# adaLN's small pieces summed four steps behind their load, and the partition sums of the larger pieces seven steps behind it

## The chip, the cores and the metric

The kernel runs on one core of a Trainium2 chip. The metric is the device time of one execution in microseconds (us). TensorE (PE) does the matmuls, VectorE (DVE), ScalarE (ACT) and GpSimd (POOL) the elementwise work. SyncE (SP) issues the transfers of the weights. The queue of ACT also issues the transfers that the change is about.

## The reference

One layer of a decoder, in float32, with 1024 tokens of width 1024. A conditioning vector c gives six modulation vectors of 1024 values each (shift, scale and gate of two sub-layers), by one product with w_ada (1024 x 6144). The modulated input goes through one wide projection into two groups of heads.

```
mod = silu(c) @ w_ada + b_ada             # six vectors: shift, scale, gate (two sub-layers)
h   = rms(x) * (1 + scale1) + shift1
rq, rk, rv, fq, fk, fv, og, rg = h @ w_in # two halves of the heads in parallel
ret = retention(rope(rq), rope(rk), rv)   # in 8 chunks of 128 tokens, state carried on
fox = softmax attention(fq, fk, fv) with forget gates, gated by og
x   = x + gate1 * ([fox, ret * gate] @ w_out)
x   = x + gate2 * (relu(h2 @ w_mlp_in)**2 @ w_mlp_out)   # h2: the second modulated norm
```

The first projection needs only shift1 and scale1. The other four vectors (numbers 2 to 5 in the code) are needed later, so their pieces of w_ada are worked off beside the projections.

## The kernel before

**Projections.** Each product is made of three matmuls of split operands (high times high, high times low, low times high; L291 to L293). The order is rq, rk, rv (retention), then fq, fk, og, fv (the attention). Each is done in two halves of four token blocks of 128, and a half has eight k-steps. So a k-step is 12 matmuls of 128x512. A half collects in four PSUM banks, and the four banks of the half after it are the ones that the half before has just filled. They come free as that half is evacuated. An evacuation of rq or rk is a copy (ACT or DVE), two rope products on POOL and two additions on DVE (L305, L354, L366 to L369). One of fq or fk is a square and a copy on ACT, a sum and a copy on DVE (L330, L333, L337). The weight of a k-step is split by ACT (L134, a cast) and DVE (L135, the low part, tile `ws`). PE can start a k-step only when that DVE operation is done.

**Retention.** Its eight chunks run beside rv half 1, fq, fk, og and fv: groups of four small matmuls on PE (rip, rop, rup, rkp and others), with operations between them on ACT, DVE and POOL.

**The pieces of adaLN.** A piece is one modulation vector's stretch of n blocks of 128 columns. Ten larger pieces have n = 2 (1 MB, tile `wa` from a pool of two buffers), and twelve small ones have n = 1 (512 KB, one buffer). A piece has three stages. `load` puts one transfer in ACT's queue (L229). `sums` multiplies the eight row blocks by c and adds them up on DVE: one L232 and seven L234. `cols_` adds over the partitions with a matmul against ones on PE (L239), and DVE adds the bias (L241). L229 and L232 keep their place in the program's order on their engines. The pieces are named wa3_0, wa3_2, ... wa2_2 (larger) and wa2_4, wa2_5, ... wa5_7 (small): the modulation vector and the block at which the piece starts. The matmuls of wa3_6 go to mps3_6.

**The order.** `plan` puts the three stages at steps of the projections: the load at step `at`, the sums `d_sum` steps later, the partition sums `d_col` steps later, at the head of that step. One step of `todo` is worked off by `ada_hook` in each k-step, from rq half 0 to fv half 0. A load of a tile whose buffer is still in use waits for the partition sums of the piece that had the buffer before. Up to fv half 0, a list scheduler with a model of the engines then decides the order on each engine. It starts from the program's order and may put an operation ahead of others when the model sees it ready. So one number of `plan` changes the order of other work too. From the attention's scores (L701) on, the order is written by hand.

Of the kernel before, what the change touches and what calls it, by code (L numbers as in the profile page):

```python
# [49 lines left out]
def tile_block(  # L50
# [170 lines left out]
    def ada_stages(m, k, n):  # L221


        w = (mr if n > 1 else ra)([P, 8, n * P], f"wa{m}_{k}")

        def load():

            at = m * D + k * P
            tc.keep_in_program_order(A.dma_start(w, wada_v[:, :, at : at + n * P]))  # L229

        def sums():
            tc.keep_in_program_order(V.tensor_scalar(w[:, 0], w[:, 0], c_act[:, 0:1], None, op0=ALU.mult))  # L232
            for j in range(1, 8):
                V.scalar_tensor_tensor(w[:, 0], w[:, j], c_act[:, j : j + 1], w[:, 0], op0=ALU.mult, op1=ALU.add)  # L234

        def cols_():
            ps = xbank(f"mps{m}_{k}")
            for i in range(n):
                T.matmul(ps[:, i : i + 1], w[:, 0, i * P : (i + 1) * P], ones, start=True, stop=True)  # L239
            at = slice(8 * m + k, 8 * m + k + n)  # L240
            V.tensor_tensor(mcol[:, at], ps[:, 0:n], bT[:, at], op=ALU.add)  # L241

        return load, sums, cols_
# [279 lines left out]
    def plan(at, n, d_sum, d_col):  # L523
        m, k = cols_left[0]
        del cols_left[:n]
        stages = []

        def begin():
            stages.extend(ada_stages(m, k, n))
            stages[0]()  # L530

        todo[at].append(begin)
        todo[at + d_sum].append(lambda: stages[1]())
        todo[at + d_col].insert(0, lambda: stages[2]())

    for n in range(10):
        plan(4 * n, 2, 4, 6)
    for n in range(12):
        plan(41 + 5 * n, 1, 3, 5)
    assert not cols_left  # L540
    todo = [[]] + todo

# [654 lines left out]
```

## Time and profile before

| what | value |
|---|---|
| runs | 1399.49, 1403.5, 1404.02 us, median 1403.5 |
| profiled execution | 1402.06 us, its span 1400.3 us |
| mean granted clock of PE | 0.983 |
| busy in the span | PE 95%, DVE 62%, POOL 43%, ACT 33% |
| adaLN's late pieces | first load at 91.1 us, last partition sum at 451.4 us |

The projections that carry these pieces take the span from about 91 to 470 us. Times below are microseconds from the start of the span, and a granted clock of 1.00 is full speed. In a row, the number in brackets is how long the engine had been idle before it, and behind the arrow stands what ended the wait.

### The profile page before, as it was taken

What the parts mean: (1) busy time and instruction counts of PE and PEld (TensorE: products, weight loads), DVE (VectorE), ACT (ScalarE), POOL (GpSimd) and SP (SyncE); (2) the same over time, 40 slices, a digit from 0 to 9 for tenths busy, and PEclk for the clock granted to TensorE, in tenths of its full rate; (3) what the DMA queues carried; (4) which work ended last, traced back from release to release, by engine and by line L of the source; (5) the groups of instructions that cost most, each with busy time, mean ns of one, the idle gap of its engine ahead of it and who ended that gap; (6) DMA issues with size and microseconds to landing.
All of it is one profiled execution on the core that took longest, in us unless ns stands there. A gap on an engine that the chain in (4) does not pass through costs nothing.

```text
span 1400.3 us, 16776 instructions
## 1 busy us (share of the span) xinstructions
PE 1330.4 (95%) x6325; PEld 1075.8 (77%) x6325; DVE 867.7 (62%) x1433; ACT 459.1 (33%) x741; POOL 599.5 (43%) x420
## 2 busy tenths in 40 slices
PE   5799999999998889999999999999999999999998
PEld 4678778878886666668877887887878788787886
DVE  6867997465564457763586927447283663827446
ACT  3342212243332357662343313223231222313222
POOL 3568452145631012232469552807337171552803
PEclk9899999999999999999999999999999999999999
DMA  9656576534357645752251211121121111211103
GB/s 271 202 118 157 153 180 136 136 91 134 115 135 177 162 117 126 244 215 76 91 181 31 75 30 31 60 61 60 31 61 47 44 61 46 75 31 30 61 8 113
DMA packets 120034, 146.09 MB, mean 104 GB/s; under 512 B 7464, under 2 KB 84344, under 8 KB 118928
## 3 DMA queue, kind: packets, MB, share of 16 engines
q1 hardware_dynamic: 97072, 128.23, 33.1%
q10 hardware_dynamic: 22880, 16.78, 3.9%
q8 instruction: 50, 0.82, 0.2%
q14 instruction: 32, 0.26, 0.1%
HBM read 122.85 MB, written 10.60 MB: 95 GB/s over the span
## 4 chain that ended last, share of the span: by engine, by line
PE 49%; DVE 4%; ACT 2%; POOL 1%; issue 1%; DMA 0%; ACTq 0%; POOLq 0%; DVEq 0%
PE X L1106 11%; PE up L1049 8%; PE up L1050 8%; PE up L1051 8%; PE Y L1106 6%; PE Z L1106 2%; PE po_woA L944 1%; PE po_woA L943 1%; PE po_woA L945 1%; ACT sa L1095 1%; DVE x L1120 1%; DVE sa L1096 1%; ACT sb L1095 1%; PE av L746 1%; POOL x L950 0%
## 5 line engine op out<-in xcount | busy, mean ns | idle before, releaser
L1049 PE MATMUL up<-h,wuh 128*128 128x512 f32 x496 | 193.1, 390 | 0.7 <-ACT h L994 0.7
L1050 PE MATMUL up<-h,wuh 128*128 128x512 f32 x496 | 193.0, 389 | 0.0
L1106 PE MATMUL X<-sb,sa 128*128 128x512 f32 x768 | 187.4, 394 | 5.4 <-ACT sb L1095 3.3
L1051 PE MATMUL up<-h,wul 128*128 128x512 f32 x496 | 192.1, 389 | 0.0
L1106 PEld LDWEIGHTS X<-sb,sa 128*128 128x128 f32 x768 | 144.2, 189 | 41.0 <-ACT sb L1095 5.8
L1096 POOL TENSOR_TENSOR sb<-wd,sb 128x1024 fp32r<-128x1024 f32 x48 | 125.1, 2607 | 65.0 <-ACT sb L1095 65.0
L1096 POOL TENSOR_TENSOR sb<-wt,sb 128x1024 fp32r<-128x1024 f32 x8 | 20.1, 2512 | 278.4 <-ACT sb L1095 278.4
L131 POOL TENSOR_TENSOR sm<-sm 128x8 f32<-128x8 f32 (+2 forms) x48 | 59.4, 1242 | 144.1 <-DVE sm L496 55.1
L1120 DVE TENSOR_TENSOR x<-X,x 128x512 f32<-128x512 f32 x128 | 84.6, 683 | 55.0 <-PE X L1106 55.0
L1096 DVE TENSOR_TENSOR sa<-u,sa 128x1024 fp32r<-128x1024 f32 x56 | 105.8, 1890 | 17.7 <-ACT sa L1095 17.7
L1049 PEld LDWEIGHTS up<-h,wuh 128*128 128x128 f32 x496 | 93.0, 188 | 20.2 <-ACT wuh L134 0.9
L1050 PEld LDWEIGHTS up<-h,wuh 128*128 128x128 f32 x496 | 93.1, 188 | 19.4 <-DVE h L995 0.2
L1051 PEld LDWEIGHTS up<-h,wul 128*128 128x128 f32 x496 | 93.1, 188 | 19.3
L1054 DVE SCALAR_TENSOR_TENSOR u<-up,rl 128x512 f32<-128x512 f32 x64 | 43.9, 687 | 98.7 <-ACT rl L1053 98.7
L135 DVE TENSOR_TENSOR wul<-wu,wuh 128x1024 fp32r<-128x1024 f32 x31 | 43.1, 1391 | 98.5 <-ACT wuh L134 91.0
L1095 ACT CAST sa<-u 128x1024 fp32r<-128x1024 f32 x56 | 58.6, 1051 | 134.6 <-PE X L1106 83.3
L1106 PE MATMUL Y<-sb,sa 128*128 128x512 f32 x384 | 91.4, 391 | 4.2 <-ACT sb L1095 4.2
L1106 PEld LDWEIGHTS Y<-sb,sa 128*128 128x128 f32 x384 | 71.6, 188 | 21.4 <-ACT sb L1095 6.8
L1095 ACT CAST sb<-wd 128x1024 fp32r<-128x1024 f32 x48 | 50.3, 1049 | 112.5 <-PE X L1106 74.8
L1071 POOL TENSOR_TENSOR wd<-wd,gf 128x1024 f32<-128x1024 f32 x32 | 83.0, 2617 | 0.8 <-DMA wd<-in_w_mlp_out_dram 0.8
L1053 ACT ACTIVATE rl<-up 128x512 f32<-128x512 f32 x64 | 38.0, 595 | 113.4 <-PE up L1051 113.3
L234 DVE SCALAR_TENSOR_TENSOR wa<-wa,sm 128x128 f32<-128x128 f32 (+1 forms) x154 | 69.4, 452 | 3.1
(285 smaller groups left out, 2953.0 us busy)
## 6 DMA issues: line engine op xcount, KB each, us to landing
wu<-in_w_mlp_in_dram SPq DMA_DIRECT2D x32, 512.0 KB, 4.1
wd<-in_w_mlp_out_dram SPq DMA_DIRECT2D x16, 1024.0 KB, 5.5
wa<-in_w_ada_dram ACTq DMA_DIRECT2D x10, 1024.0 KB, 6.0
wam<-in_w_ada_dram SPq DMA_DIRECT2D x16, 512.0 KB, 7.3
wa<-in_w_ada_dram ACTq DMA_DIRECT2D x12, 512.0 KB, 6.9
x<-in_x_dram SPq DMA_DIRECT2D x8, 512.0 KB, 7.3
wr_rq<-in_w_in_dram SPq DMA_DIRECT2D x8, 512.0 KB, 5.3
wr_rk<-in_w_in_dram SPq DMA_DIRECT2D x8, 512.0 KB, 4.0
```

The source lines that it names most:

```text
L131: G.tensor_tensor(ap, ap, mhalf.to_broadcast([P, n]), op=ALU.pow)
L135: eng.tensor_tensor(l_ap, raw_ap, f32(h_ap), op=ALU.subtract)
L234: V.scalar_tensor_tensor(w[:, 0], w[:, j], c_act[:, j : j + 1], w[:, 0], op0=ALU.mult, op1=ALU.add)
L1049: T.matmul(ps, wh[:, k, :], hh, start=(k == 0), stop=False)
L1050: T.matmul(ps, wh[:, k, :], hl, start=False, stop=False)
L1051: T.matmul(ps, wl[:, k, :], hh, start=False, stop=(k == NK - 1))
L1054: V.scalar_tensor_tensor(u, ps, 0.0, rl, op0=ALU.max, op1=ALU.mult)
L1071: gated = G.tensor_tensor(w, w, gf, op=ALU.mult)
L1095: A.copy(s[:, 0], v)
L1096: eng.tensor_tensor(s[:, 1], v, f32(s[:, 0]), op=ALU.subtract)
L1106: T.matmul(banks[i], sa[:, pa, a, ii], sb[:, pb_, a, :], start=(first and a == 0 and m == 0), stop=(a == 1 and m == 2), skip_group_check=n ...
L1120: V.tensor_tensor(xs, banks[i], xs, op=ALU.add)
```

## The change

Two numbers of the table change. The larger pieces keep their load and their sums at the same steps, and their partition sums stand one step later. The small pieces keep their load and partition sums, and their DVE sums stand one step later.

```
     for n in range(10):
-        plan(4 * n, 2, 4, 6)
+        plan(4 * n, 2, 4, 7)
     for n in range(12):
-        plan(41 + 5 * n, 1, 3, 5)
+        plan(41 + 5 * n, 1, 4, 5)
```

The engines' order shows what the scheduler makes of it. The first place is PE at the end of rq half 1 (pp_rq_7 is its last bank) and the start of rk. Before:

```order
L293 MATMUL pp_rq_6_1008<-ws_rq1_7_1140,hT7_443 128x512
L291 MATMUL pp_rq_7_1012<-ws_rq1_7_1140,hT7_443 128x512
L292 MATMUL pp_rq_7_1012<-ws_rq1_7_1140,hT7_443 128x512
L293 MATMUL pp_rq_7_1012<-ws_rq1_7_1140,hT7_443 128x512
L451 MATMUL rqp0_1731<-ident_63,rq0_939 128x128 x4
L239 MATMUL mps3_6_1251<-sm_71,wa3_6_1102 128x1 x2
L291 MATMUL pp_rk_0_1193<-ws_rk0_0_1190,hT0_162 128x512
L292 MATMUL pp_rk_0_1193<-ws_rk0_0_1190,hT0_162 128x512
```

After the change the same place on PE reads as follows (mps3_4 is the piece before mps3_6):

```order
L293 MATMUL pp_rq_6_1008<-ws_rq1_7_1136,hT7_443 128x512
L291 MATMUL pp_rq_7_1012<-ws_rq1_7_1136,hT7_443 128x512
L292 MATMUL pp_rq_7_1012<-ws_rq1_7_1136,hT7_443 128x512
L293 MATMUL pp_rq_7_1012<-ws_rq1_7_1136,hT7_443 128x512
L239 MATMUL mps3_4_1184<-sm_71,wa3_4_1024 128x1 x2
L451 MATMUL rqp0_1731<-ident_63,rq0_935 128x128 x4
L291 MATMUL pp_rk_0_1193<-ws_rk0_0_1190,hT0_162 128x512
L292 MATMUL pp_rk_0_1193<-ws_rk0_0_1190,hT0_162 128x512
```

And mps3_6 now stands on PE between the k-steps 3 and 4 of rk half 0:

```order
L291 MATMUL pp_rk_3_1205<-ws_rk0_3_1251,hT3_283 128x512
L292 MATMUL pp_rk_3_1205<-ws_rk0_3_1251,hT3_283 128x512
L293 MATMUL pp_rk_3_1205<-ws_rk0_3_1251,hT3_283 128x512
L239 MATMUL mps3_6_1266<-sm_71,wa3_6_1102 128x1 x2
L291 MATMUL pp_rk_0_1193<-ws_rk0_4_1272,hT4_324 128x512
```

So mps3_6 moved by four k-steps. Likewise mps4_6 now stands behind step 3 of rv half 0 (before: ahead of step 0), and mps2_0 behind step 7 of rv half 0 (before: behind step 6). On ACT the loads of wa3_6, wa4_2, wa4_6 and wa2_2, which need the buffers that those matmuls read, stand behind the cast of step 7 of a half instead of step 4.

The second place is DVE around the change from fq half 1 to fk half 0. L333 and L337 on fq_4 to fq_7 evacuate fq half 1. Before:

```order
L135 TENSOR_TENSOR ws_fk0_2_2632<-wr_fk0_2_2630,ws_fk0_2_2632 128x512
L232 TENSOR_SCALAR wa5_0_2477<-wa5_0_2477,sm_71 128x128
L234 SCALAR_TENSOR_TENSOR wa5_0_2477<-wa5_0_2477,sm_71 128x128
L495 TENSOR_REDUCE sm_71<-ro3_2181 128x4
L234 SCALAR_TENSOR_TENSOR wa5_0_2477<-wa5_0_2477,sm_71 128x128
L496 SCALAR_TENSOR_TENSOR sm_71<-sm_71 128x4
L234 SCALAR_TENSOR_TENSOR wa5_0_2477<-wa5_0_2477,sm_71 128x128 x3
L135 TENSOR_TENSOR ws_fk0_3_2659<-wr_fk0_2_2630,ws_fk0_3_2659 128x512
L498 TENSOR_TENSOR ro3_2181<-rop3_2147,sm_71 128x512
L234 SCALAR_TENSOR_TENSOR wa5_0_2477<-wa5_0_2477,sm_71 128x128
L337 TENSOR_REDUCE sm_71<-sq_fq4_2528 128x8
L333 COPY fq1_2284<-pp_fq_4_2331 128x2x128
```

After the change, DVE at the same place:

```order
L232 TENSOR_SCALAR wa2_7_2350<-wa2_7_2350,sm_71 128x128
L234 SCALAR_TENSOR_TENSOR wa2_7_2350<-wa2_7_2350,sm_71 128x128
L135 TENSOR_TENSOR ws_fk0_2_2632<-wr_fk0_2_2630,ws_fk0_2_2632 128x512
L234 SCALAR_TENSOR_TENSOR wa2_7_2350<-wa2_7_2350,sm_71 128x128 x3
L464 TENSOR_TENSOR rkT3_2119<-rip3_2121,tri_68 128x512
L234 SCALAR_TENSOR_TENSOR wa2_7_2350<-wa2_7_2350,sm_71 128x128
L487 TENSOR_TENSOR rst3_2161<-rup3_2156,rst2_2049 128x512
L234 SCALAR_TENSOR_TENSOR wa2_7_2350<-wa2_7_2350,sm_71 128x128 x2
L135 TENSOR_TENSOR ws_fk0_3_2659<-wr_fk0_2_2630,ws_fk0_3_2659 128x512
L337 TENSOR_REDUCE sm_71<-sq_fq4_2528 128x8
L333 COPY fq1_2276<-pp_fq_4_2331 128x2x128
```

The sums ahead of the evacuation are those of the piece before (wa2_7 in place of wa5_0); those of wa5_0 follow behind the evacuation. The third place is PE at the same boundary. Between the last matmul of fq half 1 and the first of fk half 0, where nothing stood before, there now stand eight matmuls of rop3 (the last two shown), four of rkp4, and the partition sums of wa2_7:

```order
L473 MATMUL rop3_2147<-rv0_1722,rkT3_2119 128x128
L475 MATMUL rop3_2147<-rst2_2049,rqT3_2087 128x128
L457 MATMUL rkp4_2218<-ident_63,rk1_1533 128x128 x4
L239 MATMUL mps2_7_2474<-sm_71,wa2_7_2350 128x1
L291 MATMUL pp_fk_0_2576<-ws_fk0_0_2573,hT0_162 128x512
```

What moved is work of retention: its chunks stand up to seven k-steps later than before, and a group of it stands ahead of fk half 1 and of og half 0 too. The sums of wa5_6, which stood behind step 1 of fv half 0 on DVE, now stand right behind the last weight of og half 1.

## Rows read from the trace of the kernel before

**Rows 1.** Page: the chain that ended last, shares by engine.

```profile
PE 49%; DVE 4%; ACT 2%; POOL 1%; issue 1%; DMA 0%; ACTq 0%; POOLq 0%; DVEq 0%
```

**Rows 2.** Windows: length; busy PE, PEld, DVE, ACT, POOL; clock; DMA share; GB/s.

```profile
132.00:224.00 92.00, 85.02 (x381) 69.32 (x379) 87.54 (x136) 19.48 (x33) 47.08 (x37) 0.98 0.63 164
224.00:302.00 78.00, 77.93 (x419) 66.78 (x419) 45.99 (x100) 26.29 (x48) 21.47 (x20) 1.00 0.53 117
302.00:460.00 158.00, 149.91 (x747) 125.46 (x746) 88.07 (x191) 51.68 (x99) 62.69 (x58) 0.97 0.50 136
```

**Rows 3.** Waits of PE from 132 to 460: us in total, times, longest.

```profile
PE mps L239 <- issue: 4.7, 3, 2.0
...
PE pp_fv L291 <- ACT sgf L386: 0.4, 1, 0.4
PE mps L239 <- DVE wa L234: 0.3, 1, 0.3
```

**Rows 4.** Timeline of PE: start, duration, instruction, idle time before it.

```profile
150.59 0.35 PE L239 MATMUL mps<-sm,wa 128*128 128x1 f32 x2 [1.98 <-issue]
...
315.61 0.80 PE L291 MATMUL pp_fk<-ws_fk,hT 128*128 128x512 f32 x1 [3.39 <-DVE fq L333]
...
433.19 0.50 PE L292 MATMUL pp_fv<-ws_fv,hT 128*128 128x512 f32 x1 [3.84 <-DVE ws_fv L135]
...
474.24 0.50 PE L701 MATMUL S<-kt,qt 128*128 128x512 f32 x1 [2.19 <-DMA qt<-wh]
```

**Rows 5.** Windows behind three of these waits, columns as in rows 2.

```profile
151.00:154.40 3.40, 3.40 (x10) 2.72 (x10) 3.40 (x4) 0.00 (x0) 2.17 (x3) 0.50 1.00 302
314.90:321.60 6.70, 5.99 (x16) 4.72 (x17) 3.25 (x10) 0.86 (x2) 5.51 (x6) 0.50 0.25 76
434.30:437.70 3.40, 3.40 (x10) 2.62 (x9) 1.35 (x3) 0.62 (x1) 1.60 (x1) 0.50 0.56 76
```

**Rows 6.** Timeline of DVE around the start of rk half 0.

```profile
145.13 0.35 DVE L232 TENSOR_SCALAR wa<-wa,sm 128x256 f32<-128x256 f32 x1
...
149.12 1.37 DVE L234 SCALAR_TENSOR_TENSOR wa<-wa,sm 128x256 f32<-128x256 f32 x1
150.41 1.75 DVE L135 TENSOR_TENSOR ws_rk<-wr_rk,ws_rk 128x512 fp32r<-128x512 f32 x1
152.09 1.28 DVE L305 COPY rq<-pp_rq 128x512 f32<-128x512 f32 x2
```

**Rows 7.** Timeline of ACT and its queue: load of wa3_6, cast of rq1_7.

```profile
131.31 0.55 ACTq L229 DMA_DIRECT2D wa<-in_w_ada_dram  x1
...
136.66 0.62 ACT L134 CAST ws_rq<-wr_rq 128x512 fp32r<-128x512 f32 x1 [2.10 <-PE pp_rq L293]
```

**Rows 8.** Line L229, all 22 loads.

```profile
DMA to landing us min/median/max: 4.2/6.0/10.2
```

**Rows 9.** Waits of DVE from 132 to 460: us in total, times, longest.

```profile
DVE wa L232 <- DMA wa<-in_w_ada_dram: 33.9, 10, 7.7
```

**Rows 10.** Timeline of DVE ahead of fk half 0 and in fv half 0.

```profile
310.47 0.29 DVE L232 TENSOR_SCALAR wa<-wa,sm 128x128 f32<-128x128 f32 x1 [4.81 <-DMA wa<-in_w_ada_dram]
...
315.14 0.42 DVE L333 COPY fq<-pp_fq 128x256 f32<-128x256 f32 x1
...
429.01 1.07 DVE L232 TENSOR_SCALAR wa<-wa,sm 128x128 f32<-128x128 f32 x1 [6.19 <-DMA wa<-in_w_ada_dram]
```

**Rows 11.** Timeline of PE in fq half 1: retention groups and wide matmuls.

```profile
299.37 1.05 PE L463 MATMUL rip<-rqT,rkT 128*128 128x128 f32 x8
300.26 1.06 PE L480 MATMUL rup<-rv,rk 128*128 128x128 f32 x8
301.07 0.48 PE L293 MATMUL pp_fq<-ws_fq,hT 128*128 128x512 f32 x1
301.39 0.40 PE L291 MATMUL pp_fq<-ws_fq,hT 128*128 128x512 f32 x1
301.62 0.39 PE L292 MATMUL pp_fq<-ws_fq,hT 128*128 128x512 f32 x1
```

## The prediction

> **What bounds the kernel now.** I read the chain that ended last first [rows 1]: PE holds 49% of it and DVE 4%, so the time is PE's, plus what PE waits for. The change moves work only between 132 and 460 us, so I next cut that stretch by stages [rows 2]. From 132 to 224, where the larger pieces are summed beside the rope work, PE is busy 85.0 of 92.0 us and DVE 87.5: both are nearly full, and DVE is the tighter. From 224 to 302 PE has nothing to gain (77.9 of 78.0). From 302 to 460 PE is idle 8.1 us of 158 while DVE has 70 to spare. PE waits there at single places, not for want of capacity.
>
> Then I asked what ends these waits [rows 3] and looked up the longest [rows 4]. Four kinds touch pieces. Three partition sums of larger pieces hold up PE for 4.7 us together, 1.98 of it at 150.59. The profile names no releaser ("issue"), but the last sum of that piece on DVE runs from 149.12 to 150.49, just ahead of the matmul [rows 6]. At 315.61 fk half 0 waits 3.39 us for the evacuation of fq, at 433.19 fv half 0 waits 3.84 us for the low part of a weight. Both times DVE had itself stood still for a small piece's load, 4.81 us up to 310.47 and 6.19 up to 429.01 [rows 10], and the evacuation or the weight was queued behind those sums. DVE loses 33.9 us in ten such waits in all [rows 9]; only these two, and 0.3 us of another [rows 3], reach PE. After three of the waits PE's granted clock is 0.50, the lower level [rows 5].
>
> **The change, part by part.** No operation is added or removed. The terms are the waits that go, the waits that come, and the order.
>
> *A, the larger pieces.* The three partition sums that waited now stand behind one to four further k-steps, so their 4.7 us go. But DVE has as much to do as before, and the stage cannot end before it: DVE is idle 92.0 - 87.5 = 4.5 us in it, which is the upper bound. The first place shows the limit: PE needs the second bank of rk half 0 soon after 150.6, and DVE's copy out of that bank runs from 152.09 [rows 6], behind the same sums as before. So most of the 1.98 us comes back as a wait for a bank; the two later ones (2.7 us) can go, since DVE's lead has grown by then. Bounds 0 and 4.5; I take 3.0, nearer the upper end because the two later waits make up 2.7 alone.
>
> *B, the start of fk.* In the new order the sums ahead of the evacuation are wa2_7's, and 13.8 us of PE's work (counted under E) lie between that load's release and fk. The 3.39 us goes, and with it the half clock of 314.9 to 321.6, where 5.99 us of matmuls would take 3.0 less [rows 5]: 6.4.
>
> *C, fv half 0.* The sums of wa5_6 now stand ahead of fv, where DVE has slack. 3.84 goes, 0.4 of a wait for ACT's sigmoid just ahead [rows 3], and half of a 3.4 us stretch at half clock, 1.7 [rows 5]: 5.9.
>
> *D.* One further wait for a small piece's sums, 0.3 [rows 3].
>
> *E, waits that come.* Whoever lets the sums slip one step puts them nearer to the boundaries. At fk half 0 PE now does, between the partition sum that frees the buffer for wa2_7 and its first matmul of fk, 37 wide matmuls at 0.23 us and five retention groups of about 1.05 us [rows 11], 13.8 us. In that time DVE must have the load (median 6.0 [rows 8]), and the run from the sums to the first copy out, 5.1 us before (310.47 to 315.56 [rows 10]) and about 0.8 more by the new order's extra weight and retention operations. That is 11.9; the addition, the issue and two ACT copies ahead of it in the queue I put at 1.1 (two operations like the cast's 0.62 [rows 7]). The margin is 0.8 us. Counted alike, it is 1.8 at fk half 1 and 1.1 at og half 0. With the longest landing, 10.2 [rows 8], PE would wait 3.4 + 2.4 + 3.1 = 8.9 us, and three falls of the clock at 1.7 each would make it 14.0. With the median landing it waits for nothing. Half of the loads land later than 6.0; spread evenly up to 10.2, they cost 3.2 in the mean, so 1.6 over all, and I add 0.7 for a clock that falls at one boundary in some four of ten. E is -2.3, with bounds 0 and -14.0. What waits behind DVE there is the evacuation, and behind that PE's banks.
>
> *F.* The first transposes that prepare the attention stand behind three more matmuls on PE, 3 x 0.23 = 0.7, and the scores wait 2.19 us for a transfer at the end of that chain [rows 4]: -0.7.
>
> The late loads of the larger pieces I cost at nothing in the sum. Before, wa3_6's load was issued at 131.31 and its sums began at 145.13. Now it stands behind the cast of rq1_7, which ended at 137.3 [rows 7], so 7.8 us are left. The sums' place on DVE hides the load if it lands within that; the median does, the longest would be 2.4 us late.
>
> Sum against the profiled execution: 1402.06 - 3.0 - 6.4 - 5.9 - 0.3 + 2.3 + 0.7 = 1389.5. The median of the runs lies 1.4 above that execution, so by the runs it would be 1390.9. I say 1390.
>
> What is granted of the clock changes A. The row shows 0.50 from 151.0 to 154.4 behind a wait of 1.98 [rows 5], and I did not count that stretch, because PE would then wait for DVE's low part of a weight instead. [...]
>
> **The rivals.** *Waits return at the boundaries.* E at its far end: the small pieces' loads land near 10 us and hold up the evacuations of three halves. For it speaks that DVE's waits for these loads are long already (7.7 us the longest, [rows 9]); against it the median of 6.0. Gain 3.0 + 12.6 - 14.0 - 0.7 = 0.9, so 1401; if only half of that comes, 1394.
>
> *The change does not do what it says.* The order is made by a model of the engines, and real waits can move from one piece to another. DVE's 33.9 us of waits speak for it: one load's latency is hidden one step more, and the next piece's load starts no earlier, since one buffer serves all the small ones. If each of the three waits that end is replaced by one as long elsewhere, the time stays at 1402.
>
> *Slower: the late loads of the larger pieces.* Four of them (wa3_6, wa4_2, wa4_6, wa2_2) have 7.8 us left instead of 13.8. They run beside SP's weights in a stage where the DMA share is 0.63 [rows 2]. Each us beyond 7.8 is a DVE stall in a stage where DVE has 4.5 us to spare. At a landing of 13 the stalls are 4 x 5.2 = 20.8, the stage loses 16.3 and A's 3.0 is gone; against that stand 12.6 - 2.3 - 0.7 = 9.6 from B to F. That ends at 1408.8. It decides from a landing of 11.3 (4 x 3.5 = 14.0, less 4.5 = 9.5); the longest seen is 10.2 [rows 8], which speaks against it.
>
> The Trainium skill speaks for this rival: DMA: Bandwidth & Descriptors, section "Queues, rings and completion order", says that each DMA engine takes turns between the queues that have work, packet by packet. A load that meets the weights would then go at half the rate. The trace shows landings of up to 10.2 where the shares are high, and no order between the queues. By the rule a 1 MB load at half of 302 GB/s would take 7 us, an estimate, and still be in time.
>
> **How the numbers follow.** The forecast has 0.56, with a range of its own of 1384 to 1397 (A at 4.5, E at 0 and the clock's 1.7 give the lower end, A at 0 and half of E's far end the upper). Waits that return have 0.17, no effect 0.13, the late loads 0.09, and 0.05 remain for a time below 1383, by waits that end and that I did not list. The range of 1383 to 1403 leaves out the late loads, that low end and a few hundredths of no effect. A change of 0.3%, 4.2 us, is about what a measurement here can tell from none. Faster by more: 0.56 + 0.05 and 0.11 of the returning waits, 0.72. Within it: 0.06 of these, and 0.12 of no effect, 0.18. Slower: 0.10.
>
> **What the changed profile would show.** For A: no "issue" wait of a partition sum between 132 and 224, and a wait of the second bank at the start of rk in its place; the stage shorter by about 3 us, DVE busy all but 1 or 2 of it. For B and C: no wait of PE of more than 1 us at the starts of fk and fv, and a clock of 1.00 there. For E: waits of L291 at fk half 1 or og half 0, behind DVE's L333 or L337, with a wait of DVE for `wa` just before. For the slower rival: waits of DVE for `wa` inside 132 to 224, where the trace of before has none. For no effect: the idle time of PE between 132 and 460 as large as before, at other lines. The forecast is wrong if loads land at 9 us or more in most steps, or if the new place of retention's groups on PE delays a half that had no wait before.

## The result, and the profile after

The changed kernel took 1391.41 us in the median of six runs (1385.8 to 1396.51), the kernel before 1402.58 in six. The ratio of the runs is 0.9928, 95% interval 0.9908 to 0.9947: 10.1 us less, 7.4 to 12.9 (the two medians lie 11.2 apart). The forecast was 12.6 less (1402.06 to 1389.5), the given time 1390. The profiled execution was the shortest of the six (1385.8 us, span 1384.1). A second profile of the same kernel, below, spans 1391.2.

Two of the three stretches of [rows 2] in the profile after (length; busy PE, PEld, DVE, ACT, POOL; clock; DMA share; GB/s):

```profile
132.00:224.00 92.00, 86.63 (x383) 70.72 (x382) 81.56 (x131) 18.84 (x33) 46.82 (x36) 0.96 0.59 160
302.00:460.00 158.00, 157.31 (x812) 132.88 (x811) 99.22 (x205) 56.08 (x104) 62.71 (x58) 1.00 0.57 152
```

From 302 to 460 PE is now idle for 0.7 us instead of 8.1, at full clock. In the first stage PE works longer but at a lower clock (0.96 against 0.98), which is no gain. DVE is busy for 81.6 us there, not 87.5, and still PE waits. All waits of PE from 132 to 460 (us in total, times, longest) show for what, against [rows 3, 4]:

```profile
PE pp_rk L292 <- DVE ws_rk L135: 2.6, 2, 2.4
PE pp_rv L291 <- DVE rk L354: 1.5, 1, 1.5
PE pp_rk L291 <- DVE rq L305: 1.3, 1, 1.3
PE pp_rv L291 <- DVE rv L305: 1.0, 1, 1.0
PE pp_og L291 <- DVE fk L333: 0.7, 1, 0.7
PE pp_rv L291 <- ACT rv L303: 0.3, 1, 0.3
```

No partition sum (mps, L239) waits any more, and the waits at fk and fv are gone; one of 0.7 us has come at og. But evacuations and low parts of weights of rk and rv have taken the place of the partition sums. The places on PE's timeline:

```profile
151.98 0.50 PE L291 MATMUL pp_rk<-ws_rk,hT 128*128 128x512 f32 x1 [1.28 <-DVE rq L305]
...
164.18 0.66 PE L292 MATMUL pp_rk<-ws_rk,hT 128*128 128x512 f32 x1 [2.38 <-DVE ws_rk L135]
...
312.78 0.49 PE L291 MATMUL pp_fk<-ws_fk,hT 128*128 128x512 f32 x1
...
462.30 0.50 PE L701 MATMUL S<-kt,qt 128*128 128x512 f32 x1 [2.04 <-DMA qt<-wh]
```

The first matmul of fk has no bracket: it waited for nothing. Windows at two places of [rows 5], and at the two falls of the clock that stand before 460 now:

```profile
164.40:167.70 3.30, 3.30 (x9) 2.52 (x9) 3.26 (x8) 0.00 (x0) 0.00 (x0) 0.50 1.00 303
201.90:205.30 3.40, 3.40 (x8) 2.74 (x9) 3.40 (x5) 0.00 (x0) 3.40 (x3) 0.50 0.98 167
314.90:321.60 6.70, 6.70 (x31) 5.52 (x31) 5.30 (x10) 1.56 (x3) 6.70 (x9) 1.00 0.38 103
434.30:437.70 3.40, 3.40 (x16) 2.82 (x15) 0.13 (x1) 0.79 (x2) 0.00 (x0) 1.00 1.00 179
```

The stretch at 314.9 holds 31 matmuls now, 16 before. Why fk does not wait is read from DVE's timeline ahead of it, against [rows 10]:

```profile
304.44 0.29 DVE L232 TENSOR_SCALAR wa<-wa,sm 128x128 f32<-128x128 f32 x1 [2.16 <-DMA wa<-in_w_ada_dram]
...
308.13 1.39 DVE L234 SCALAR_TENSOR_TENSOR wa<-wa,sm 128x128 f32<-128x128 f32 x2
...
310.05 0.67 DVE L337 TENSOR_REDUCE sm<-sq_fq 128x8 f32<-128x512 f32 x1
310.65 0.41 DVE L333 COPY fq<-pp_fq 128x256 f32<-128x256 f32 x1
```

The first copy out ends at 311.06, PE arrives at 312.78: 1.7 us to spare, where the prediction counted 0.8. DVE's wait for the load is 2.2 us instead of 4.8. Over the stretch from 132 to 460 DVE waits less for the loads, and the landings that the view of L229 gives lie closer together, against [rows 8, 9]:

```profile
DVE wa L232 <- DMA wa<-in_w_ada_dram: 20.5, 8, 5.1
```

```profile
DMA to landing us min/median/max: 5.4/5.8/7.6
```

That view, here and in [rows 8], does not hold all 22 loads: the trace ties only six of them to a landing here, and seven before. The load that is summed ahead of fk is not among them. It was issued at 300.29, and its sums began at 304.44, when it had come: 4.2 us, less than the smallest of the view.

```profile
300.29 0.55 ACTq L229 DMA_DIRECT2D wa<-in_w_ada_dram  x1
```

### The profile page after: what moved, and what is told of

Its sections match the earlier page's. It is cut to its first block, busy times and chain, and to the rows that moved or that the text cites. A ratio compares the mean times of both kernels' runs of the same rounds, so it can differ in the third digit from the quotient of the medians.

```text
span 1384.1 us, 16774 instructions
## 1 busy us (share of the span) xinstructions
PE 1322.4 (96%) x6325; PEld 1070.1 (77%) x6325; DVE 869.4 (63%) x1433; ACT 460.4 (33%) x741; POOL 601.6 (43%) x420
## 4 chain that ended last, share of the span: by engine, by line
PE 50%; DVE 4%; ACT 2%; POOL 1%; issue 1%; DMA 0%; ACTq 0%; POOLq 0%; DVEq 0%
PE X L1106 11%; PE up L1049 8%; PE up L1050 8%; PE up L1051 8%; PE Y L1106 6%; PE Z L1106 2%; PE po_woA L944 1%; PE po_woA L943 1%; PE po_woA L945 1%; ACT sa L1095 1%; DVE x L1120 1%; DVE sa L1096 1%; ACT sb L1095 1%; PE av L746 1%; POOL x L950 0%
```

## The experiments

The order of twelve runs: first each edit alone and the two stalls one by one, then the larger pieces' stage and the distance, last the second profile and DVE's load. Each ratio is to the kernel before, measured on the same chip.

**The larger pieces' edit alone (e1).**

```
         plan(4 * n, 2, 4, 7)
-        plan(41 + 5 * n, 1, 4, 5)
+        plan(41 + 5 * n, 1, 3, 5)
```

> Only the larger pieces' partition sums one step later, the small pieces as before. The theory (the gain is from the two stalls at fk half 0 and fv half 0, and the larger pieces' waits only change their name because the additions of rope hold up DVE): 1 us less than before at most 2, so about 1401.5, fk half 0 and fv half 0 still wait 3 to 4 us each, and in rk half 0 PE waits 2 us or more for the low part of the weight of k-step 4. The prediction's term A: 3.0 us less, 1399.5. A rival by which the larger pieces carry the change: 6 us less or more.

Measured: 1404.68 us, ratio 1.0025 (1.0010 to 1.0040), 3.5 us more. None of the times expected came: the edit costs time. All its waits of PE from 132 to 460 above 1 us in total:

```profile
PE pp_fv L292 <- DVE ws_fv L135: 3.8, 1, 3.8
PE pp_fk L291 <- DVE fq L333: 3.5, 1, 3.5
PE pp_rk L292 <- DVE ws_rk L135: 3.3, 3, 1.4
PE pp_rv L291 <- DVE rv L305: 1.7, 1, 1.7
PE mps L239 <- DVE wa L234: 1.7, 2, 1.2
PE pp_rv L291 <- DVE rk L354: 1.1, 1, 1.1
PE pp_rk L291 <- DVE rk L354: 1.1, 1, 1.1
```

The two stalls of the small pieces are where they were. In the larger pieces' stage the 4.7 us of partition sums are gone (the 1.7 of the list stand at 423 and 456 us), and waits for weights and evacuations have grown by more: in rk and rv they now come to 9.0 us. DVE also stands still for 1.4 us there until the input of its scan has landed, which the kernel before does not show. In the kernel before PE's waits for weights and evacuations came to 2.4:

```profile
PE pp_rk L292 <- DVE ws_rk L135: 1.0, 1, 1.0
PE pp_rv L291 <- DVE rk L354: 0.7, 1, 0.7
PE pp_rk L291 <- DVE rk L354: 0.7, 1, 0.7
```

**The small pieces' edit alone (e2).**

```
-        plan(4 * n, 2, 4, 7)
+        plan(4 * n, 2, 4, 6)
         plan(41 + 5 * n, 1, 4, 5)
```

> Only the small pieces' DVE sums one step later, the larger pieces as before. The theory: nearly the whole of the change, 9.5 to 11 us less than before, about 1392, with no wait of PE above 1 us between 302 and 460 and the three waits of partition sums between 132 and 224 as before. A rival by which the two edits need each other: 6 us or less.

Measured: 1390.36 us, ratio 0.9919 (0.9901 to 0.9936), 11.4 us less (9.0 to 13.9). As the theory expected, it is the whole change. Of the partition sums between 132 and 224 two still wait, 3.1 us together. Between 302 and 460 PE waits 0.9 us at og and 1.0 in fv, and nowhere longer.

**One piece, wa2_6 (e3), and the last seven (e8).** Larger pieces as before; the line with the minus is that of the kernel before.

```
-        plan(41 + 5 * n, 1, 3, 5)
+        plan(41 + 5 * n, 1, 4 if n == 2 else 3, 5)
```

> The DVE sums one step later for one small piece alone, wa2_6, whose delay puts wa2_7's sums in the place of wa5_0's ahead of the evacuation of fq. The theory: the wait of 3.39 us at fk half 0 and the half clock behind it go, 6.4 us less, about 1396; the wait of 3.84 us in fv half 0 stays. A rival by which any new order of retention's groups gives the gain and the single stall does not: less than 2 us, or the stall comes back at another boundary between 300 and 400.

```
-        plan(41 + 5 * n, 1, 3, 5)
+        plan(41 + 5 * n, 1, 4 if n > 4 else 3, 5)
```

> The DVE sums one step later for the last seven small pieces alone (wa5_1 to wa5_7), so that wa5_6's stand ahead of fv half 0. The theory: the 3.84 us in fv half 0, 0.4 just ahead and the half clock behind go, 5.9 us less, about 1396.7; the wait of 3.39 us at fk half 0 stays as before. The rival: less than 2 us, or the wait comes back at og or fv.

Measured: e3 1399.07, ratio 0.9978 (0.9965 to 0.9991), 3.1 us less; e8 1393.9, ratio 0.9940 (0.9923 to 0.9958), 8.4 us less. Together 11.5, as much as e2. In e8 only fk's stall is left from 300 to 460:

```profile
PE pp_fk L291 <- DVE fq L333: 3.3, 1, 3.3
```

In e3 the wait at fk shrank from 3.39 to 2.14 us and did not go. DVE and PE there:

```profile
307.76 0.29 DVE L232 TENSOR_SCALAR wa<-wa,sm 128x128 f32<-128x128 f32 x1 [2.42 <-DMA wa<-in_w_ada_dram]
...
313.41 0.41 DVE L333 COPY fq<-pp_fq 128x256 f32<-128x256 f32 x1
```

```profile
313.88 0.50 PE L291 MATMUL pp_fk<-ws_fk,hT 128*128 128x512 f32 x1 [2.14 <-DVE fq L333]
```

From the sums' start to the end of the first copy out DVE takes 6.1 us here (307.76 to 313.82) and 6.6 in the changed kernel (304.44 to 311.06). So the changed kernel's DVE is no quicker. Its PE comes later: 8.3 us behind the sums' start, here 4.0 (311.74, without the wait, less 307.76). Retention's groups, the third place of the order, stand ahead of fk there and not here. In the changed kernel they begin at 310.42:

```profile
310.42 0.38 PE L473 MATMUL rop<-rv,rkT 128*128 128x128 f32 x2
```

With the partition sum behind them they last until 312.78, which is 2.4 of the 4.4 us. The other 2.0 is a load that comes earlier against the end of fq. Without the groups PE would have come 6.0 us behind the sums' start and waited some 0.6, an estimate from these rows. So it takes both there to leave no wait.

**The scan out of the way, with both edits (e4) and with the small pieces' edit (e5).**

```
-    forget_cumsum()
     proj_block("rk", OFF_R + RW, evac_rope("rk"), ada_hook)
...
     proj_group("rv", OFF_R + 2 * RW, 1, evac_rv, ret_hook(2))
+    forget_cumsum()
     proj_group("fq", 0, 0, evac_fox("fq"), ret_hook(2))
```

The reason is seen in the changed kernel's DVE rows in rk half 0:

```profile
151.25 0.68 DVE L305 COPY rq<-pp_rq 128x512 f32<-128x512 f32 x1
151.85 2.27 DVE L434 TENSOR_TENSOR_SCAN cc<-sm,cc 8x1024 f32<-8x1024 f32 x1
154.05 0.65 DVE L305 COPY rq<-pp_rq 128x512 f32<-128x512 f32 x1
...
160.64 1.49 DVE L368 TENSOR_TENSOR rq<-ac_rq,as_rq 128x256 f32<-128x256 f32 x1 [2.44 <-POOL as_rq L367]
...
163.45 0.68 DVE L135 TENSOR_TENSOR ws_rk<-wr_rk,ws_rk 128x512 fp32r<-128x512 f32 x1
```

The scan stands between the two copies out, DVE then waits 2.44 us for POOL, and the weight for which PE waits at 164.18 is queued behind.

> The changed kernel with the forget gates' running sum (a scan of 2.27 us on DVE, L434) called behind rv instead of between rq and rk. The theory: the edit of the larger pieces costs 1 to 3 us because the scan came ahead of a copy out of a bank, so POOL's rope products, DVE's additions behind them and the weight of k-step 4 of rk are late; without the scan there PE's wait of 2.4 us in rk half 0 and the half clock behind it go, 3 to 4 us less than the changed kernel, about 1388. The rival, that DVE's work on rope sets that stage with or without the scan: less than 1 us, and the wait comes back at another k-step of rk.

> The kernel with the edit of the small pieces alone, and the scan called behind rv. The theory: there the scan stood between rope additions and cost PE about 1 us, so 1 to 2 us less than with the small pieces' edit alone, about 1389, and within 2 us of the kernel with both edits and the moved scan. If the larger pieces' edit is worth its 3.0 us once the scan is out of the way (the prediction's term A), it is 3 us slower than that kernel.

Measured: e4 1392.66, ratio 0.9924 (0.9906 to 0.9942); e5 1389.03, ratio 0.9904 (0.9886 to 0.9922). In e4 the wait at k-step 4 of rk is down to 0.34 us and the clock does not fall from 132 to 460, as expected. But PE waits 1.45 us for a weight at the start of rk, 2.12 for rk's evacuation and 1.65 for rv's (the first of these stands in the changed kernel's second profile too, e9, with 1.44), and the time is that of the changed kernel. So the scan explains that one wait and not the loss: the rival held. With the scan away the kernel with the larger pieces' edit is still 2.8 us slower by the middles of the ratios (0.9924 against 0.9904), which the intervals do not tell from nothing.

**The larger pieces' sums later still (e6), with the small pieces as changed.**

```
-        plan(4 * n, 2, 4, 7)
+        plan(4 * n, 2, 4, 8)
```

> The changed kernel with the larger pieces' partition sums at eight steps instead of seven, so their loads come later by another step. The theory: within 3 us of the changed kernel (1388 to 1395), PE's waits in 132 to 224 again by the weights' low parts and the evacuations. The prediction's rival of late loads: DVE waits for these loads inside 132 to 224 by 2 us or more a piece, and the time is above 1398.

Measured: 1400.98, ratio 0.9988 (0.9978 to 0.9998). The time is that of the late loads, the cause is not: DVE waits for no load of a piece between 132 and 224 (1.7 us for its scan's input). The clock of that stretch is 0.94, in the changed kernel 0.96. PE's waits from 132 to 460 begin with

```profile
PE mps L239 <- issue: 7.7, 4, 2.7
PE pp_rq L292 <- DVE ws_rq L135: 3.3, 1, 3.3
```

The scheduler put the DVE sums of these pieces later as well, so PE waits for partition sums again, and once for a weight behind sums.

**The small pieces' sums earlier (e7).**

```
         plan(4 * n, 2, 4, 6)
-        plan(41 + 5 * n, 1, 3, 5)
+        plan(41 + 5 * n, 1, 2, 5)
```

> The larger pieces as before, the small pieces' DVE sums one step earlier than before (2 instead of 3 behind the load). The theory: DVE meets more loads that have not landed, its waits for them grow from 34 us to 45 or more and the stalls at fk half 0 and fv half 0 stay: 1402 to 1410. The rival by which any shuffle of the order takes the stalls away: 1397 or less.

Measured: 1389.9, ratio 0.9906 (0.9891 to 0.9921), 13.2 us less. The theory fell here, as far as it was one of distance: DVE's waits for loads came to 28.2 us, not to 45 or more, and the stalls did not stay. All PE waits from 132 to 460:

```profile
PE mps L239 <- issue: 3.5, 2, 2.0
PE pp_rk L292 <- DVE ws_rk L135: 0.9, 1, 0.9
PE pp_rv L291 <- DVE rk L354: 0.7, 1, 0.7
PE pp_rk L291 <- DVE rk L354: 0.6, 1, 0.6
PE rmp L505 <- POOL ro L501: 0.2, 1, 0.2
```

None is left at fk or fv. DVE's rows ahead of fk show why: the evacuation comes first, and the piece that stood there before begins its sums behind it.

```profile
312.56 0.68 DVE L337 TENSOR_REDUCE sm<-sq_fq 128x8 f32<-128x512 f32 x1
313.16 0.41 DVE L333 COPY fq<-pp_fq 128x256 f32<-128x256 f32 x1
...
322.48 0.28 DVE L232 TENSOR_SCALAR wa<-wa,sm 128x128 f32<-128x128 f32 x1
```

**The changed kernel again (e9).** No edit.

> The changed kernel once more, for a second profile beside the first, whose execution was the shortest of its six. By the runs so far: 1391 (1389 to 1393). If the first profile is typical, fq starts about 1 us earlier than before (256.4); if the edit of the larger pieces costs time, as the kernel with it alone showed, fq starts 1 us or more later than before (258.5 or more).

Measured: 1393.09, ratio 0.9938 (0.9919 to 0.9957). The second profile has waits at the same places in rk and rv, 7.8 us in all (6.7 in the first), and 1.0 us for a cast in fv, behind which the clock falls. The largest from 132 to 460:

```profile
PE pp_rk L292 <- DVE ws_rk L135: 3.9, 2, 2.4
PE pp_rv L291 <- DVE rk L354: 1.5, 1, 1.5
PE pp_rv L291 <- DVE rv L305: 1.3, 1, 1.3
PE pp_fv L291 <- ACT ws_fv L134: 1.0, 1, 1.0
```

fq starts at 258.28 there, 256.43 in the first profile, 257.45 in the kernel before. That lies 0.2 us short of the 258.5 that would have spoken for a cost. The nearer comparison is e2, where retention's groups stand as in the changed kernel: fq starts at 257.14 there, so the first profile is 0.7 us ahead of it and the second 1.1 behind. One profile cannot settle the sign.

**Copies out of the banks on ACT, with the small pieces' edit (e10) and with both (e11).**

```
-        if t % 2 == 0:
-            A.copy(dst, src)
-        else:
-            V.tensor_copy(dst, src)
+        A.copy(dst, src)
```

> The kernel with the small pieces' edit alone, and all plain copies out of the banks of rq and rv on ACT instead of every second one on DVE. It takes eight copies of about 0.65 us off DVE in the stage of the larger pieces, where both engines are nearly full. DVE's queue as the limit of that stage: 1 to 3 us less than the small pieces' edit alone, 1387 to 1389. If POOL's rope products set it: no difference.

> The changed kernel with the same copies on ACT. The theory that the larger pieces' edit gains nothing because PE then waits for DVE's evacuations and weights: with DVE relieved the edit is worth its waits again, and this is 1 to 3 us below the small pieces' edit with the copies on ACT. The rival, that the later sums are the loss whatever DVE has to do: 1 us or more above it.

Measured: e10 1389.14, ratio 0.9908 (0.9892 to 0.9925); e11 1391.59, ratio 0.9919 (0.9901 to 0.9937). With DVE relieved the kernel with the larger pieces' edit still gains nothing, some 1.5 us more by the middles, within the intervals. The pair is not clean: the scheduler also orders retention's groups differently in e11. The copies themselves may save 1.5 us (e10 against e2), within the intervals.

**What gained, put together (e12).** The larger pieces as before.

```
-        plan(41 + 5 * n, 1, 3, 5)
+        plan(41 + 5 * n, 1, 2, 5)
...
-    forget_cumsum()
     proj_block("rk", OFF_R + RW, evac_rope("rk"), ada_hook)
...
+    forget_cumsum()
     proj_group("fq", 0, 0, evac_fox("fq"), ret_hook(2))
```

> The version put together from what gained: larger pieces as before, the small pieces' sums two steps behind their load, the scan called behind rv. If the gains add up (1.5 us for the scan in the kernel with the small pieces' edit, 12.5 for the earlier sums): about 1387.5, below all kernels so far. If the new order of the one undoes the other: a wait of 2 us or more of PE at fk half 0 or fv half 0, 1392 or more.

Measured: 1386.8, ratio 0.9893 (0.9875 to 0.9911), the fastest of all, 15.0 us less than before. Its only wait of PE above 0.7 us between 224 and 460 is at 459.53, for the attention's first transfer.

## Why the prediction came out right, and where not

The time and the direction held; the sum got there by errors that cancel in part, so its closeness is partly luck.

- **A, -3.0, was wrong in sign.** The step that failed is "the two later ones (2.7 us) can go, since DVE's lead has grown by then". Alone the edit cost 3.5 us (1.4 to 5.6), and in the three other pairs (e2 with the changed kernel and e9, e5 with e4, e10 with e11) the kernel with it was 1.3 to 2.8 us slower by the middles, though no single one of these is beyond its intervals. The first half of A's working held: the wait at the start of rk came back as one for a bank (1.28 of 1.98; in the second profile as 0.27 for a bank and 1.44 for a weight). But the rest came back too, for evacuations L354 and L305 and for weights. It looks as if the partition sums had stood where PE would have waited for DVE anyway; that was argued from the places, not tried. DVE is idle for 10.4 us of the stage after (92.0 - 81.6), where the prediction expected 1 or 2: its work does not fill the stage, and 92.0 - 87.5 did not measure what there was to gain. PE still waits for single operations that stand behind others in DVE's queue and behind POOL's rope products. What exactly makes the edit a loss rather than a zero stays open; the scan (e4) and the copies (e10, e11) are not it alone.
- **B to F, -9.6 in sum, was right**: -11.4 (9.0 to 13.9) measured. By single stalls it was off both ways: B 6.4 predicted and 3.1 with one piece moved, where 2.14 us of the wait stayed; C 5.9 predicted and 8.4.
- **E, +2.3, was too much, and its margins were too.** In the first profile only og waits, 0.7 us (0.5 in the second), with no fall of the clock behind it. At fk PE's work behind the partition sum took 12.8 us (299.98 to 312.78), not 13.8, and DVE's run 6.6, not 5.9; the 1.7 us to spare came from a load that took 4.2 us, not 6.0. At og the load took at most 6.3 (issued at 355.12, summed from 361.41), and PE waited 0.7 where 1.1 was counted as spare with a load of 6.0. The spread of landings up to 10.2, on which the 1.6 rests, was read from seven loads and not from 22.
- **F, +0.7, is not seen**: the scores wait 2.04 us, before 2.19.
- **The late loads** were right to cost nothing: no wait of DVE for a piece's load stands between 132 and 224, in the changed kernel or in e6. It was close: wa3_6's load was issued at 136.29 and landed 7.5 us later, 0.4 ahead of its sums at 144.25. By the Trainium skill (DMA: Bandwidth & Descriptors, "Queues, rings and completion order") a DMA engine takes turns between the queues that have work, packet by packet, and the estimate from it was 7 us for 1 MB. The trace agrees for wa3_6 and not for wa4_2, 1 MB as well, which landed after 5.4 us; that queues took turns no run here shows.
- **The clock behind 151** was left in the sum at 0.50 for one stretch. It stayed at 1.00 there and fell behind 164.18 and 201.87 instead: two stretches where the sum had one, and by the prediction's own count a stretch costs 1.7 us. No run shows the 1.7 us less of the range's lower end as a gain: in e4 the clock did not fall from 132 to 460, and the time was that of the changed kernel.
- **The cause, as the prediction had it, was too narrow.** It saw the evacuation and the weight queued behind the sums that wait, but took the gain from a load that is released further ahead of fk and fv; the theory of e7 was the same distance. e7 has the sums nearer to their loads and gains as much. What e3, e7 and e8 share with the changed kernel is the place: PE stops where a small piece's sums, waiting for their load, stand on DVE ahead of what the next half needs (an evacuation, or the low part of a weight). In e7 the evacuation comes first, and by its rows that is enough: the first copy out ends at 313.57, before the groups of retention that stand ahead of fk there too (from 313.85). In the changed kernel the earlier load and the groups together give PE what it needs. That the groups alone would do it was not tried.

## What to carry to other kernels

When an engine in order waits for a load, look at what is queued behind the wait. If it is something that another engine needs at the change from one stage to the next, moving the wait either way past it is worth the stall and the clock lost behind it; here 11 to 13 us, from one number. A wait that is the last of several in a row may be worth nothing by itself, as the partition sums here: before counting it, look up when the next operand of the same engine is ready. And an engine's idle share in a stage does not tell what the stage can gain while single operations in its queue stand behind others.

## What the runs showed that was not expected

The clock fell behind a wait of 1.52 us (at 201.87 in the changed kernel), and not behind one of 2.12 us in e4 or of 1.28 at 151.98. So the length of the single wait did not decide it.

Two executions of the same program differed by 1.9 us at the start of fq, by 4.2 at the scores (462.30 and 466.45) and by 7.1 in the span (1384.1 and 1391.2). Behind the scores, where the change moves nothing, the first took 921.8 us, the second 924.7 and the kernel before 926.1 (474.24 to 1400.3). The clock differs there. The same window before, after and in the second profile, columns as in rows 2:

```profile
475.00:525.00 50.00, 43.27 (x239) 31.86 (x238) 26.50 (x86) 24.34 (x54) 5.80 (x20) 0.90 0.48 123
475.00:525.00 50.00, 43.71 (x292) 31.81 (x293) 33.51 (x112) 32.51 (x69) 9.16 (x24) 0.97 0.62 144
475.00:525.00 50.00, 42.90 (x269) 30.56 (x268) 32.44 (x109) 31.03 (x65) 6.09 (x21) 0.93 0.52 120
```

So of the 16.2 us between the first profile and the one before, 4.3 lie behind all that the change moves, and the first profile flatters it. The six runs of the changed kernel spread over 10.7 us. A sum of terms of 1 us each cannot be told from the times here, only from the waits.
